# A transformer layer on one core: up to LayerNorm 1, products with a weight piece in two runs, the high part's first and the low part's second

## The chip, the core and the metric

The kernel runs on one core of a Trainium2 chip. A core has five engines with queues of their own: TensorE (PE, matrix products, with its weight loads shown as PEld), VectorE (DVE), ScalarE (ACT), GpSimd (POOL) and SyncE (SP), which here issues the transfers. They wait for each other by semaphores. The metric is the device time of one execution in microseconds (us).

## What is computed

One layer of a diffusion transformer, in float32: 256 latent tokens and 256 context tokens of width 2048, 16 heads of 128. The reference, cut to what matters:

```python
sh1, sc1, g1, sh2, sc2, g2 = ada_mods(c, w_ada[layer], b_ada[layer])
qa, ka, va, qb, kb, vb = mixer_qkv(modulate(x, sh1, sc1), w_in[layer], q_norm_g[layer], k_norm_g[layer], rope)
qac, kac, vac, qbc, kbc, vbc = mixer_qkv(modulate(ctx, csh1, csc1), w_in[layer], q_norm_g[layer], k_norm_g[layer], None)
heads = jnp.concatenate([window_sink_attention(qa, ka, va, kac, vac, sink_logit[layer]),
                         global_attention(qb, kb, vb, kbc, vbc)], axis=-1)
x = layer_norm(DN_ALPHA * x + g1 * (heads @ w_out[layer]), ln1_g[layer], ln1_b[layer])
x = layer_norm(DN_ALPHA * x + g2 * swiglu(modulate(x, sh2, sc2), w_gate[layer], w_up[layer], w_down[layer]),
               ln2_g[layer], ln2_b[layer])
```

`ada_mods` gives shifts, scales and gates: silu of the conditioning vector times `w_ada`. `mixer_qkv` is one product of the modulated tokens with `w_in`, split into queries, keys and values of two head groups.

## The kernel before

**Products in three parts.** A float32 product is made of three products in the faster format F32R. The token operand is split into a high part (a cast) and a low part (the operand minus its high part), and so is the weight. With token parts xh, xl and weight parts hi, lo the kernel adds hi·xh, lo·xh and hi·xl into one accumulator bank of PSUM; `mm3` (L340 to 343) issues them in this order. A weight piece is two blocks of 128 rows by 512 columns: it is loaded by SP into a `raw` buffer, ACT casts `hi` from it (L603), and DVE takes the difference `lo` (L606). The rows of the profile with `hi`, `lo`, `uh`, `ul` (modulated input) and `oTh`, `oTl` (attention output) are these.

**Two halves.** Up to LayerNorm 1 (conditioning columns, q/k/v products, attention, output product) the order of the work is planned: each piece of work is a step of the class `Flow`, with an engine, a supposed duration, the steps that it follows, and the rooms (buffers) that it takes and gives back. `Flow.search` tries orders by a list schedule with random ranks from a fixed seed and keeps the one with the earliest supposed end; `Flow.run` then issues the steps in that order, on all five engines. From LayerNorm 1 on (`pb`, L1462) the code's own order holds: gate and up projections, down projection, LayerNorm 2.

**The steps of a weight piece.** `flow_weights` makes, for each piece, ACT's cast and DVE's difference. The cast takes one room `hl` for both parts (four rooms, `HL_BUFS`); the difference gives back the raw buffer. Pieces loaded ahead for the last output columns (`spare`) take two rooms of the pool `b4` instead. `flow_products` makes one PE step for one piece and one row block of 128 tokens: for one or two weight blocks `mm3`, so three or six products. The step waits for the cast, for the difference (200 ns less), for the operand's high part and its low part (400 ns less), and for the row's step before; it gives back the weight room and both operand rooms. `flow_block` calls it for the q/k/v columns (two row blocks for a query block, four for a key/value block, pieces outside and rows inside), `flow_out` for the output product (two row blocks; with `by_tile` rows outside and pieces inside).

**Work beside them on the planned path.** `flow_columns` (PE, L654) multiplies the conditioning vector with pieces of `w_ada`; `flip` (L755) turns the input, L984 and L937 queries and keys; scores, row maxima (L1031), exponentials (L1043), weighing (L1056), a way through DRAM that turns the probabilities, and the values (L1081) make the attention; L1414 is one more conditioning product at the end of the stage, and `z_flip` (L1445) turns LayerNorm 1's output of the first row block, twice two blocks. Behind that ACT modulates (L1666), casts `u2h` (L1668) and DVE takes `u2l` (L1669) for the first gate products.

Of the kernel before, what the change touches and what calls it, by code (L numbers as in the profile page):

```python
# [14 lines left out]
F32R = mybir.dt.float32r  # L15
# [8 lines left out]
P = 128  # L24
# [4 lines left out]
NT = SEQ // P  # L29
# [237 lines left out]
def dit_layer(ctx: ExitStack, tc: tile.TileContext, x, c, cx, c_ctx, w_ada, b_ada, w_in, q_norm_g,  # L267
              k_norm_g, sink_logit, w_out, ln1_g, ln1_b, w_gate, w_up, w_down, ln2_g, ln2_b,
              rope_cos, rope_sin, out):
    nc = tc.nc  # L270
    x, c, cx = x[0], c, cx[0]
# [4 lines left out]
    whl = ctx.enter_context(tc.tile_pool(name="whl", bufs=HL_BUFS))  # L276
# [63 lines left out]
    def mm3(ps, xh, xl, w, first, last, seeded=False):  # L340
        nc.tensor.matmul(ps, lhsT=xh, rhs=w[0], start=first, stop=False, skip_group_check=seeded)  # L341
        nc.tensor.matmul(ps, lhsT=xh, rhs=w[1], start=False, stop=False, skip_group_check=seeded)  # L342
        nc.tensor.matmul(ps, lhsT=xl, rhs=w[0], start=False, stop=last, skip_group_check=seeded)  # L343
# [28 lines left out]
    araw = ea.enter_context(tc.tile_pool(name="araw", bufs=ADA_BUFS))  # L372
# [172 lines left out]
    def b4(shape, dtype, name):  # L547
        return pa.tile(shape, dtype, tag="b4", name=name, bufs=NB4)
# [39 lines left out]
    def flow_weights(w, k0, nk, c0, width=NB, where=("raw", "araw"), spare=False, small=False, behind=(None, None)):  # L588

        raw, ld = flow_load(w, k0, nk, c0, width, where, small=small)  # L590
        pieces = []
        for s in range(0, nk * width, SUB * NB):
            n = min(SUB * NB, nk * width - s)
            hl = Buf("b4" if spare else "hl")
            hl.rooms = [hl, Buf("b4")] if spare else [hl]

            def cast(hl=hl, s=s, n=n):
                if spare:
                    hl.hi, hl.lo = (b4([P, SUB * NB], F32R, c) for c in ("hi", "lo"))
                else:  # L600
                    hl.hi = whl.tile([P, SUB * NB], F32R, tag="hi", name="hi")
                    hl.lo = whl.tile([P, SUB * NB], F32R, tag="lo", name="lo")
                nc.scalar.copy(hl.hi[:, :n], raw.t[:, s : s + n])  # L603

            def rest(hl=hl, s=s, n=n):
                nc.vector.tensor_tensor(hl.lo[:, :n], raw.t[:, s : s + n], hl.hi[:, :n].bitcast(F32), op=ALU.subtract)  # L606
# [101 lines left out]
    u = {}  # L708
# [94 lines left out]
    def flow_block(g, b, chunks):  # L803


        k0, ng = GROUPS[g]
        kvi = {2: 0, 5: 1}.get(b)
        gi = {0: 0, 1: 1, 3: 2, 4: 3}.get(b)
        rows = range(2 if kvi is None else 4)
        accs = [Buf("acc") for r in rows]  # L810
        sums = [qacc[gi][r] if kvi is None else kvacc[kvi][r // 2][:, r % 2, :] for r in rows]
        ends = {r: flow_seed(accs[r], lambda r=r: sums[r], [evacs[b, r], chunks[0][0][1][0]]) for r in rows} if g >= SEED_G else {}
        done = 0
        for (hl, deps), cols in chunks:
            kk = k0 + done
            base = kk - (kk - k0) % G4
            for r in rows:
                rooms, steps = u[base, r // 2]
                j0 = kk - base

                def operand(j, rooms=rooms, r=r):
                    tt = slice((r % 2) * P, (r % 2) * P + P)
                    return rooms[0].t[:, j, tt], rooms[1].t[:, j, tt]

                xs = [lambda j=j0 + i, f=operand: f(j) for i in range(len(cols))]
                ends[r] = flow_products(hl, deps, steps[j0 // 2], cols, accs[r], xs, done == 0,
                                        done + len(cols) == ng, ends.get(r))
                for m in rooms:
                    m.left += 1
                    ends[r].give.append(m)  # L830
            done += len(cols)
        for r in rows:
            eng = "ACT" if g >= SEED_G or g == 0 and not (r % 2 or b < 2) else "DVE"

            def evac(dst=sums[r], ps=accs[r], eng=eng):
                if eng == "ACT":
                    nc.scalar.copy(dst, ps.t)
                elif g > 0:
                    nc.vector.tensor_add(dst, dst, ps.t)
                else:  # L840
                    nc.vector.tensor_copy(dst, ps.t)

            evacs[b, r] = F.add(eng, 520 if eng == "ACT" else 710 if g < 3 else 615, evac, [ends[r], evacs.get((b, r))], give=[accs[r]])
# [386 lines left out]
    def flow_out(gs, n, by_tile=False):  # L1230
# [9 lines left out]
        def products(gi, i, piece, t):  # L1240
            hl, deps = piece
            rooms, ready = oT[gi]

            def operand(j):
                return rooms[0].t[:, j, t * P : (t + 1) * P], rooms[1].t[:, j, t * P : (t + 1) * P]

            xs = [lambda j=2 * i + c: operand(j) for c in range(2)]
            ends[t] = s = flow_products(hl, deps, ready[t][2 * i : 2 * i + 2], [0, NB], accs[t], xs,
                                        (gi, i) == (gs[0], 0), (gi, i) == (gs[-1], 1), ends.get(t))
            for m in rooms:  # L1250
                m.left += 1
                s.give.append(m)
# [733 lines left out]
```

## Time and profile before

| | |
|---|---|
| Three runs | 1122.13, 1122.73 and 1122.84 us, median 1122.73 |
| Profiled execution, first to last instruction | 1121.0 us |
| Mean granted TensorE clock | 0.996 |
| ACT busy | 598.7 us, 53% |
| High parts up to LayerNorm 1 (L603) | 86 casts, 87.4 us, 1030 ns each |
| Low parts up to LayerNorm 1 (L606) | 86 differences, 101.3 us, 1194 ns each |
| Products hi·xh with the modulated input (L341) | 256, 405 ns each |
| PE idle behind DVE's low part there (L342) | 0.6 us |
| HBM read over the span | 304.07 MB |

The profile shows one execution. Times are us from the first instruction, durations in the groups are means of one instruction in ns. A row of the timeline gives start, duration, engine, line, operation, output<-inputs, and in brackets the idle time before it and what ended it. "PE busy" counts products that overlap each other, and their ends are modelled.

### The profile page before, as it was taken

What the parts mean: (1) busy time and instruction counts of PE and PEld (TensorE: products, weight loads), DVE (VectorE), ACT (ScalarE), POOL (GpSimd) and SP (SyncE); (2) the same over time, 40 slices, a digit from 0 to 9 for tenths busy, and PEclk for the clock granted to TensorE, in tenths of its full rate; (3) what the DMA queues carried; (4) which work ended last, traced back from release to release, by engine and by line L of the source; (5) the groups of instructions that cost most, each with busy time, mean ns of one, the idle gap of its engine ahead of it and who ended that gap; (6) DMA issues with size and microseconds to landing.
All of it is one profiled execution on the core that took longest, in us unless ns stands there. A gap on an engine that the chain in (4) does not pass through costs nothing.

```text
span 1121.0 us, 14130 instructions
## 1 busy us (share of the span) xinstructions
PE 1102.3 (98%) x5213; PEld 883.7 (79%) x5213; DVE 903.4 (81%) x1133; ACT 598.7 (53%) x875; POOL 36.7 (3%) x82
## 2 busy tenths in 40 slices
PE   8999999999999999999999999999999999999995
PEld 6766688777887788888888878888888888888884
DVE  5763589899999888787778697988996987689876
ACT  3341554878685356444475565767766344444442
POOL 1000030110100001000000000000000000000000
PEclk9999999999999999999999999999999999999998
DMA  9999999778999778999956677777776998669742
GB/s 321 394 385 375 393 362 377 247 234 274 345 332 395 249 269 321 348 318 296 336 182 216 223 220 266 234 246 271 228 267 216 329 348 293 228 235 379 287 149 76
DMA packets 178317, 321.26 MB, mean 287 GB/s; under 512 B 8732, under 2 KB 43196, under 8 KB 175943
## 3 DMA queue, kind: packets, MB, share of 16 engines
q1 hardware_dynamic: 177528, 320.03, 81.7%
q8 instruction: 41, 0.67, 0.2%
q10 hardware_dynamic: 720, 0.33, 0.1%
q14 instruction: 28, 0.23, 0.1%
HBM read 304.07 MB, written 16.25 MB: 286 GB/s over the span
## 4 chain that ended last, share of the span: by engine, by line
PE 91%; DMA 3%; DVE 2%; ACT 1%; SPq 1%; issue 0%; ACTq 0%; DVEq 0%
PE acc L341 20%; PE acc L343 20%; PE acc L342 20%; PE wk L342 8%; PE wk L341 8%; PE wk L343 8%; PE wk L1081 2%; PE wk L654 2%; DMA raw<-in_w_in_dram 2%; DVE lo L332 1%; DMA lgb<-in_ln_g_dram 1%; PE wk L755 1%; SPq L569 1%; DMA xt<-in_x_dram 0%; PE wk L1414 0%
## 5 line engine op out<-in xcount | busy, mean ns | idle before, releaser
L331 ACT CAST hi<-raw 128x1024 fp32r<-128x1024 f32 x279 | 290.7, 1054 | 256.4 <-PE acc L343 162.4
L332 DVE TENSOR_TENSOR lo<-raw,hi 128x1024 fp32r<-128x1024 f32 x279 | 336.1, 1220 | 103.6 <-ACT hi L331 101.4
L341 PE MATMUL acc<-hi,u2h 128*128 128x512 f32 x390 | 152.5, 391 | 0.0
L343 PE MATMUL acc<-hi,u2l 128*128 128x512 f32 x390 | 151.7, 390 | 0.7 <-DVE u2l L1669 0.7
L342 PE MATMUL acc<-lo,u2h 128*128 128x512 f32 x390 | 151.8, 389 | 0.0
L603 ACT CAST hi<-raw 128x1024 fp32r<-128x1024 f32 (+1 forms) x86 | 87.4, 1030 | 113.8 <-DMA raw<-in_w_in_dram 63.2
L466 DVE SCALAR_TENSOR_TENSOR adav<-raw,cs,adav 128x512 f32<-128x512 f32 (+1 forms) x128 | 121.4, 949 | 8.4 <-DMA raw<-in_w_ada_dram 4.9
L606 DVE TENSOR_TENSOR lo<-raw,hi 128x1024 fp32r<-128x1024 f32 (+1 forms) x86 | 101.3, 1194 | 16.3 <-ACT hi L603 15.5
L341 PE MATMUL acc<-hi,uh 128*128 128x512 f32 x256 | 103.7, 405 | 1.3 <-ACT uh L769 0.8
L342 PE MATMUL wk<-lo,u2h 128*128 128x512 f32 x264 | 103.1, 390 | 0.5 <-DVE lo L332 0.5
L343 PE MATMUL wk<-hi,u2l 128*128 128x512 f32 x264 | 102.7, 389 | 0.0
L341 PE MATMUL wk<-hi,u2h 128*128 128x512 f32 x264 | 102.2, 389 | 0.0
L342 PE MATMUL acc<-lo,uh 128*128 128x512 f32 x256 | 100.5, 392 | 0.6 <-DVE lo L606 0.6
L343 PE MATMUL acc<-hi,ul 128*128 128x512 f32 x256 | 100.1, 391 | 0.4 <-DVE ul L784 0.4
L341 PE MATMUL acc<-hi,hTh 128*128 128x512 f32 x236 | 92.0, 390 | 0.4 <-ACT acc L1901 0.4
L342 PE MATMUL acc<-lo,hTh 128*128 128x512 f32 x236 | 91.8, 389 | 0.0
L343 PE MATMUL acc<-hi,hTl 128*128 128x512 f32 x236 | 91.8, 389 | 0.0
L343 PEld LDWEIGHTS acc<-hi,u2l 128*128 128x128 f32 x390 | 73.2, 188 | 16.2 <-DVE u2l L1669 1.1
L341 PEld LDWEIGHTS acc<-hi,u2h 128*128 128x128 f32 x390 | 73.2, 188 | 16.1 <-ACT u2h L1668 0.8
L342 PEld LDWEIGHTS acc<-lo,u2h 128*128 128x128 f32 x390 | 73.2, 188 | 15.1
L341 PEld LDWEIGHTS acc<-hi,uh 128*128 128x128 f32 x256 | 48.1, 188 | 19.0 <-issue 5.6
L342 PEld LDWEIGHTS wk<-lo,u2h 128*128 128x128 f32 x264 | 49.5, 188 | 12.0 <-DVE lo L332 1.8
(277 smaller groups left out, 1748.0 us busy)
## 6 DMA issues: line engine op xcount, KB each, us to landing
raw<-in_w_ada_dram SPq DMA_DIRECT2D x70, 1024.0 KB, 7.7
raw<-in_w_gate_dram SPq DMA_DIRECT2D x44, 1024.0 KB, 6.7
raw<-in_w_up_dram SPq DMA_DIRECT2D x44, 1024.0 KB, 5.6
raw<-in_w_down_dram SPq DMA_DIRECT2D x44, 1024.0 KB, 5.8
raw<-in_w_ada_dram SPq DMA_DIRECT2D x48, 512.0 KB, 5.9
raw<-in_w_in_dram SPq DMA_DIRECT2D x18, 1024.0 KB, 11.0
raw<-in_w_out_dram SPq DMA_DIRECT2D x16, 1024.0 KB, 6.5
pd<-hx SPq DMA_DIRECT2D x64, 128.0 KB, 3.4
```

Of the source, the lines that this page charges most:

```text
L331: nc.scalar.copy(hi[:, :n], raw[:, s : s + n])
L332: nc.vector.tensor_tensor(lo[:, :n], raw[:, s : s + n], hi[:, :n].bitcast(F32), op=ALU.subtract)
L341: nc.tensor.matmul(ps, lhsT=xh, rhs=w[0], start=first, stop=False, skip_group_check=seeded)
L342: nc.tensor.matmul(ps, lhsT=xh, rhs=w[1], start=False, stop=False, skip_group_check=seeded)
L343: nc.tensor.matmul(ps, lhsT=xl, rhs=w[0], start=False, stop=last, skip_group_check=seeded)
L466: nc.vector.scalar_tensor_tensor(a[:, c : c + piece], raw[:, f : f + piece], cs[:, 4 * (g * (G4 * NB // w) + j) + 2, None], a[:, c : c + p ...
L569: nc.sync.dma_start(room.t, w[k0 * P : (k0 + 1) * P, c0 : c0 + width])
L603: nc.scalar.copy(hl.hi[:, :n], raw.t[:, s : s + n])
L606: nc.vector.tensor_tensor(hl.lo[:, :n], raw.t[:, s : s + n], hl.hi[:, :n].bitcast(F32), op=ALU.subtract)
L654: nc.tensor.matmul(bank.t[32 * j : 32 * j + 32, :width], lhsT=cs[:, 4 * k + 2 - 2 * i : 4 * k + 34 - 2 * i], rhs=raw.t[:, c * width : (c + ...
L755: nc.tensor.transpose(ps.t[:, (j * 2 + t) * P : (j * 2 + t + 1) * P], src, ident)
L1081: nc.tensor.matmul(o_ps.t[:, : 2 * P].rearrange("p (g q) -> p g q", q=32), lhsT=v, rhs=pv[:, k], start=k == 0, stop=k == 3)
```

## The change

The room `hl` becomes two, `hi` and `lo`, four of each as before. The cast takes the high room only; the difference takes the low room when DVE comes to it, and the tile is made there. The PE step of a piece and a row block becomes two: the high run (hi·xh and hi·xl for each block, two or four products) and the low run (lo·xh, one or two). The high run waits for the cast and for the operand's parts (the low one 200 ns less), and gives back the high room and the operand's low room; the low run waits for its own high run and for the difference, and gives back the low room and the operand's high room. In `flow_block` the high runs of all row blocks of a piece are named first and then the low runs, in `flow_out` too, except with `by_tile`, where each low run follows its high run. The order in which they are named is a rank for the planner, not the order of the program. The rest of the code, past LayerNorm 1 too, is the same; its lines move by up to 12.

```diff
-    F = Flow({"raw": RAW_BUFS, "araw": ADA_BUFS, "hl": HL_BUFS, "acc": 4, ...
+    F = Flow({"raw": RAW_BUFS, "araw": ADA_BUFS, "hi": HL_BUFS, "lo": HL_BUFS, "acc": 4, ...
...
-            hl = Buf("b4" if spare else "hl")
-            hl.rooms = [hl, Buf("b4")] if spare else [hl]
+            hl = Step()
+            hl.rooms = [Buf("b4"), Buf("b4")] if spare else [Buf("hi"), Buf("lo")]
...
-            a = F.add("ACT", 60 + 0.87 * n, cast, [ld, behind[0]], hl.rooms)
-            b = F.add("DVE", 60 + 1.06 * n, rest, [a, behind[1]], give=[raw])
+            a = F.add("ACT", 60 + 0.87 * n, cast, [ld, behind[0]], hl.rooms[:1])
+            b = F.add("DVE", 60 + 1.06 * n, rest, [a, behind[1]], hl.rooms[1:], [raw])
...
-        after = [deps[0], (deps[1], 200), ready[0], (ready[1], 400), prev]
-        return F.add("PE", 681 * len(cols), fn, after, [ps] if first and not seed else [], list(hl.rooms))
+        def high():
+            if first and not seed:
+                ps.t, ps.seeded = acc_bank(), False
             for i, (c, x) in enumerate(zip(cols, xs)):
+                for j, h in enumerate(x()):
+                    nc.tensor.matmul(ps.t, lhsT=h, rhs=hl.hi[:, c : c + NB], start=first and not seed and i == j == 0,
+                                     stop=False, skip_group_check=ps.seeded)
+
+        def low():
+            for i, (c, x) in enumerate(zip(cols, xs)):
+                nc.tensor.matmul(ps.t, lhsT=x()[0], rhs=hl.lo[:, c : c + NB], start=False,
+                                 stop=last and i == len(cols) - 1, skip_group_check=ps.seeded)
+
+        a = F.add("PE", 454 * len(cols), high, [deps[0], ready[0], (ready[1], 200), prev],
+                  [ps] if first and not seed else [], hl.rooms[:1])
+        return a, lambda: F.add("PE", 227 * len(cols), low, [a, deps[1]], [], hl.rooms[1:])
...
-                ends[r] = flow_products(hl, deps, steps[j0 // 2], cols, accs[r], xs, done == 0,
-                                        done + len(cols) == ng, ends.get(r))
-                for m in rooms:
-                    m.left += 1
-                    ends[r].give.append(m)
+                a, lows[r] = flow_products(hl, deps, steps[j0 // 2], cols, accs[r], xs, done == 0,
+                                           done + len(cols) == ng, ends.get(r))
+                rooms[1].left += 1
+                a.give.append(rooms[1])
+            for r in rows:
+                rooms = u[base, r // 2][0]
+                ends[r] = lows[r]()
+                rooms[0].left += 1
+                ends[r].give.append(rooms[0])
```

**The opening on TensorE.** The first products of the kernel, with the first piece of w_in; `acc`, `hi`, `lo`, `uh` and `ul` carry the numbers of their tiles. Before:

```order
L391 MATMUL wk_96<-ident_70 128x128 x4
L341 MATMUL acc_245<-hi_221,uh_233 128x512
L342 MATMUL acc_245<-lo_222,uh_233 128x512
L343 MATMUL acc_245<-hi_221,ul_234 128x512
L341 MATMUL acc_253<-hi_221,uh_233 128x512
L342 MATMUL acc_253<-lo_222,uh_233 128x512
L343 MATMUL acc_253<-hi_221,ul_234 128x512
```

Now (L629 are high products, L634 low ones):

```order
L391 MATMUL wk_96<-ident_70 128x128 x4
L629 MATMUL acc_246<-hi_223,uh_235 128x512
L629 MATMUL acc_246<-hi_223,ul_236 128x512
L629 MATMUL acc_251<-hi_223,uh_235 128x512
L629 MATMUL acc_251<-hi_223,ul_236 128x512
L634 MATMUL acc_246<-lo_233,uh_235 128x512
```

The product with the low part of the input has moved from the third place to the second, the one with the low part of the weight to the fifth.

**The piece of w_in near 102 us on TensorE.** Behind two groups of conditioning products comes the first piece of the next w_in load. Before:

```order
L654 MATMUL wk_938<-raw_903,cs_106 32x512 x4
L654 MATMUL wk_938<-raw_958,cs_106 32x512 x4
L1381 MATMUL wk_1009<-ident_70,lrow_153 128x32
L341 MATMUL acc_1011<-hi_999,uh_832 128x512
L342 MATMUL acc_1011<-lo_1000,uh_832 128x512
L343 MATMUL acc_1011<-hi_999,ul_833 128x512
```

Now the same place ends its sixteen high products (four row blocks, four each, the last four shown) with:

```order
L629 MATMUL acc_1022<-hi_991,ul_864 128x512
L629 MATMUL acc_1027<-hi_991,uh_863 128x512
L629 MATMUL acc_1027<-hi_991,ul_864 128x512
L629 MATMUL acc_1027<-hi_991,uh_863 128x512
L629 MATMUL acc_1027<-hi_991,ul_864 128x512
L634 MATMUL acc_1008<-lo_1006,uh_839 128x512 x2
```

The first product with the low part stood second; now sixteen others are ahead of it.

**VectorE in the attention stretch, now.** Rows with what each waits for: `lo` are differences of weight pieces, `hx` turned probabilities, `m` row maxima, `nm` and `es` what the exponentials need.

```order
L603 TENSOR_TENSOR lo<-raw,hi 128x1024 [waits PE_49]
L1070 STREAM_TRANSPOSE hx<-pr 128x4x4x32 [waits Activation_49]
L1038 TENSOR_REDUCE m<-wk 128x1
L603 TENSOR_TENSOR lo<-raw,hi 128x1024 [waits DMAHW5_49,PE_49,Activation_49]
L1043 SCALAR_TENSOR_TENSOR nm<-m,nsink 128x2 [waits DVE_49]
L1044 TENSOR_TENSOR es<-nm,nsink 128x2 [waits DVE_49]
```

The waits for PE in the rows of `lo` stood with ACT's cast of the same piece before; of 86 such rows 36 have one now, and 4 had one.

**The end of the stage on TensorE.** The last output products, the conditioning products L1414 (now L1426) and the flips of LayerNorm 1's output L1445 (now L1457), up to the first gate product. Before:

```order
L343 MATMUL acc_3493<-hi_3345,oTl_3260 128x512
L1414 MATMUL wk_3664<-raw_3535,cs_106 32x512 x4
L1445 MATMUL wk_3670<-ident_70,xt_76 128x128 x2
L1414 MATMUL wk_3664<-raw_3551,cs_106 32x512 x4
L1445 MATMUL wk_3679<-ident_70,xt_76 128x128 x2
L1414 MATMUL wk_3664<-raw_3567,cs_106 32x512 x4
L1414 MATMUL wk_3664<-raw_3584,cs_106 32x512 x4
L341 MATMUL acc_3724<-hi_3614,u2h_3696 128x512
```

Now:

```order
L1426 MATMUL wk_3655<-raw_3530,cs_106 32x512 x4
L634 MATMUL acc_3509<-lo_3442,oTh_3254 128x512 x2
L1426 MATMUL wk_3655<-raw_3550,cs_106 32x512 x4
L1426 MATMUL wk_3655<-raw_3567,cs_106 32x512 x4
L1426 MATMUL wk_3655<-raw_3583,cs_106 32x512 x4
L1457 MATMUL wk_3684<-ident_70,xt_76 128x128 x2
L1457 MATMUL wk_3688<-ident_70,xt_76 128x128 x2
L341 MATMUL acc_3724<-hi_3594,u2h_3696 128x512
```

All conditioning products have moved ahead of both flips. ACT's first modulation reads `wk_3670` before and `wk_3688` now.

More of the change, by code (lines that the diff above doesn't have):

```diff
@@ L537, in dit_layer @@
     fill(pa, 448)
-    F = Flow({"raw": RAW_BUFS, "araw": ADA_BUFS, "hl": HL_BUFS, "acc": 4, "wk": 4, "b4": NB4, "t2k": T2K},
+    F = Flow({"raw": RAW_BUFS, "araw": ADA_BUFS, "hi": HL_BUFS, "lo": HL_BUFS, "acc": 4, "wk": 4, "b4": NB4, "t2k": T2K},
              {"SP": 1800.0, "PE": 6300.0, "ACT": 5100.0, "DVE": 4200.0, "POOL": 4000.0})
@@ L593, in flow_weights @@
             n = min(SUB * NB, nk * width - s)
-            hl = Buf("b4" if spare else "hl")
-            hl.rooms = [hl, Buf("b4")] if spare else [hl]
+            hl = Step()
+            hl.rooms = [Buf("b4"), Buf("b4")] if spare else [Buf("hi"), Buf("lo")]
             def cast(hl=hl, s=s, n=n):
[L598 to L602, printed above, removed]
+                hl.hi = b4([P, SUB * NB], F32R, "hi") if spare else whl.tile([P, SUB * NB], F32R, tag="hi", name="hi")
                 nc.scalar.copy(hl.hi[:, :n], raw.t[:, s : s + n])
             def rest(hl=hl, s=s, n=n):
+                hl.lo = b4([P, SUB * NB], F32R, "lo") if spare else whl.tile([P, SUB * NB], F32R, tag="lo", name="lo")
                 nc.vector.tensor_tensor(hl.lo[:, :n], raw.t[:, s : s + n], hl.hi[:, :n].bitcast(F32), op=ALU.subtract)
-            a = F.add("ACT", 60 + 0.87 * n, cast, [ld, behind[0]], hl.rooms)
-            b = F.add("DVE", 60 + 1.06 * n, rest, [a, behind[1]], give=[raw])
+            a = F.add("ACT", 60 + 0.87 * n, cast, [ld, behind[0]], hl.rooms[:1])
+            b = F.add("DVE", 60 + 1.06 * n, rest, [a, behind[1]], hl.rooms[1:], [raw])
             pieces.append((hl, (a, b)))
@@ L625, in flow_products @@
         seed = first and prev is not None
-        def fn():
+        def high():
             if first and not seed:
@@ L630, in fn @@
             for i, (c, x) in enumerate(zip(cols, xs)):
-                xh, xl = x()
-                mm3(ps.t, xh, xl, (hl.hi[:, c : c + NB], hl.lo[:, c : c + NB]),
-                    first and not seed and i == 0, last and i == len(cols) - 1, ps.seeded)
-        after = [deps[0], (deps[1], 200), ready[0], (ready[1], 400), prev]
-        return F.add("PE", 681 * len(cols), fn, after, [ps] if first and not seed else [], list(hl.rooms))
+                for j, h in enumerate(x()):
[8 more added lines that the diff above has]
+        return a, lambda: F.add("PE", 227 * len(cols), low, [a, deps[1]], [], hl.rooms[1:])
     last_load, first_sum = [], []
@@ L816, in flow_block @@
             base = kk - (kk - k0) % G4
+            lows = {}
             for r in rows:
@@ L1247, in products, with finish @@
             xs = [lambda j=2 * i + c: operand(j) for c in range(2)]
[L1248 to L1252, printed above, removed]
+            a, low = flow_products(hl, deps, ready[t][2 * i : 2 * i + 2], [0, NB], accs[t], xs,
+                                   (gi, i) == (gs[0], 0), (gi, i) == (gs[-1], 1), ends.get(t))
+            rooms[1].left += 1
+            a.give.append(rooms[1])
+            def finish():
+                ends[t] = s = low()
+                rooms[0].left += 1
+                s.give.append(rooms[0])
+            return finish
         if by_tile:
@@ L1256, in flow_out @@
                 for p in pieces:
-                    products(*p, t)
+                    products(*p, t)()
         else:
             for p in pieces:
-                for t in range(NT):
-                    products(*p, t)
+                run([products(*p, t) for t in range(NT)])
         def finish(t):
```

## The prediction

> **What bounds the kernel now.** I read the page's shares and its chain first, then the busy time by stretch, then the order of time around every place where TensorE (PE) stands still.
>
> ```profile
> PE 1102.3 (98%) x5213; PEld 883.7 (79%) x5213; DVE 903.4 (81%) x1133; ACT 598.7 (53%) x875; POOL 36.7 (3%) x82
> PE 91%; DMA 3%; DVE 2%; ACT 1%; SPq 1%; issue 0%; ACTq 0%; DVEq 0%
> 100.00:120.00 20.00, 19.44 (x115) 11.99 (x113) 6.14 (x10) 2.58 (x3) 0.00 (x0) 1.00 1.05 405
> 160.00:180.00 20.00, 20.00 (x90) 16.57 (x89) 19.61 (x24) 13.72 (x19) 2.02 (x4) 1.00 1.04 414
> 260.00:280.00 20.00, 18.51 (x84) 14.72 (x83) 19.03 (x39) 17.23 (x42) 0.00 (x0) 1.00 0.81 265
> ```
>
> TensorE sets the time: 98% busy, 91% of the chain. In the stretches (columns: us; busy us of PE, PEld, DVE, ACT, POOL; granted clock; DMA share; GB/s) the clock is 1.00 throughout. Between 160 and 180 us VectorE (DVE) is busy for 19.61 of 20 us too, and the DMA share is full: nothing has much room.
>
> A busy PE hides small waits, though. A 512-column product is shown 0.39 us long, but the next begins after 0.227:
>
> ```profile
> 265.22 0.39 PE L343 MATMUL acc<-hi,oTl 128*128 128x512 f32 x1
> ...
> 267.94 0.39 PE L343 MATMUL acc<-hi,oTl 128*128 128x512 f32 x1
> 269.62 0.50 PE L341 MATMUL wk<-kTh,qTh 128*128 128x512 f32 x1 [1.29 <-ACT pr L1043]
> ...
> 271.11 0.40 PE L342 MATMUL acc<-lo,oTh 128*128 128x512 f32 x1
> 271.71 0.50 PE L343 MATMUL acc<-hi,oTl 128*128 128x512 f32 x1 [0.20 <-DVE oTl L1093]
> 272.04 0.40 PE L341 MATMUL acc<-hi,oTh 128*128 128x512 f32 x1
> ```
>
> Twelve products stand between the first two rows: 2.72 / 12 = 0.227 us each. So a wait is read from start to start. The step from 267.94 to 269.62 is 1.68 us, 1.45 too long, though the row says 1.29; and a product behind a wait is followed after 0.33, 0.11 too late. The second wait (271.11 to 271.71) costs 0.60 - 0.23 + 0.11 = 0.48. The two make 1.45 + 0.11 + 0.48 = 2.0 us, the largest loss of the attention stretch. The change can win such waits and nothing else: it takes no product away.
>
> **The change, part by part.** *Same work.* A triple (high·high, low·high, high·low) becomes two products in the high run and one in the low run, each 0.227 us, with as many casts, differences and transfers. Weight loads stay one for each product (x5213 against x5213) and lie beside products (16.57 of 20 us). Zero from the rows; the bounds are zero too, as no form of instruction is new.
>
> *The order is drawn anew.* The planner is a seeded random search over its steps. There are more steps now, so all five engines' orders up to LayerNorm 1 differ, also where no weight piece is involved. The sum therefore goes by places.
>
> *The opening*, from the rows of before:
>
> ```profile
> 14.14 0.50 PE L341 MATMUL acc<-hi,uh 128*128 128x512 f32 x1 [0.79 <-ACT uh L769]
> 14.48 0.41 PE L342 MATMUL acc<-lo,uh 128*128 128x512 f32 x1
> 14.83 0.43 DVE L784 TENSOR_TENSOR ul<-uf,uh 128x256 fp32r<-128x256 f32 x1
> 15.31 0.50 PE L343 MATMUL acc<-hi,ul 128*128 128x512 f32 x1 [0.42 <-DVE ul L784]
> 16.09 0.69 DVE L841 COPY kvacc<-acc 128x512 f32<-128x512 f32 x1
> 16.69 3.16 DVE L606 TENSOR_TENSOR lo<-raw,hi 128x1024 fp32r<-128x1024 f32 x3
> 20.50 0.50 PE L341 MATMUL acc<-hi,uh 128*128 128x512 f32 x1 [0.43 <-DVE kvacc L841]
> 21.39 0.32 PE L654 MATMUL wk<-raw,cs 128*32 128x128 f32 x4
> ```
>
> In before the first wait is for the low part of the input (`ul`, ready at 14.83 + 0.43 = 15.26), and the low weight product runs ahead of it. Now `ul` is needed by the second product: at 15.31 one product is done instead of two. The other wait, for an accumulator that DVE empties, comes a product group earlier: DVE now takes the three differences before its first copy, so from 16.09, where the copy began, they end at 16.09 + 3.16 = 19.25 and the copy at 19.25 + 0.69 = 19.95; PE waits from 19.3 to about 20.1, and six products are left. The conditioning products (L654 in before) then start at 20.1 + 0.34 + 5 × 0.227 + 0.1 = 21.65 instead of 21.39. I take **+0.3**; bounds -0.3 (both waits half as long) and +0.9 (both in full again).
>
> *The late w_in piece at 102 us.*
>
> ```profile
> 100.89 1.99 ACT L603 CAST hi<-raw 128x1024 fp32r<-128x1024 f32 x2 [11.58 <-DMA raw<-in_w_in_dram]
> ...
> 101.97 2.36 DVE L606 TENSOR_TENSOR lo<-raw,hi 128x1024 fp32r<-128x1024 f32 x2 [1.00 <-ACT hi L603]
> ...
> 102.20 0.49 PE L341 MATMUL acc<-hi,uh 128*128 128x512 f32 x1
> 103.25 0.50 PE L342 MATMUL acc<-lo,uh 128*128 128x512 f32 x1 [0.56 <-DVE lo L606]
> 103.59 0.40 PE L343 MATMUL acc<-hi,ul 128*128 128x512 f32 x1
> ```
>
> The high part is there just in time; the difference takes 1.2 us more and PE stands. In the new order sixteen high products (16 × 0.227 = 3.6 us) stand between, so the wait goes: 103.59 - 102.20 - 2 × 0.227 = 0.94. I take **-0.9**; bounds -0.9 and 0 (if the piece lands so much later that PE waits for the high part). What would be late next is the second difference at 101.97 + 2.36 = 104.3; its products come later still.
>
> *The attention stretch.* Here the change adds a wait. The low room was taken together with the high room, by ScalarE's (ACT's) cast; now DVE takes it when it comes to the difference. In the order with waits 36 of the 86 differences wait for PE, where 4 did. Queued behind each are the row maxima, the subtractions for the next operands and the copies out of accumulators, and PE waits for all of these. ACT is relieved: the high room comes back before the low run.
>
> ```profile
> ACT hi L603 <- PE acc L343: 41.4, 27, 10.7
> ...
> 265.65 1.06 ACT L603 CAST hi<-raw 128x1024 fp32r<-128x1024 f32 x1 [0.67 <-PE acc L343]
> 266.60 1.33 ACT L1056 ACTIVATE pr<-pr,ll 128x512 f32<-128x512 f32 x2
> ...
> 268.72 0.76 ACT L1043 ACTIVATE pr<-wk,nm,qsc 128x512 f32<-128x512 f32 x1
> ```
>
> The first row (view of waits: us, times, longest) prices such a wait at 41.4 / 27 = 1.5 us of the waiting engine. The others show when it reaches PE: ACT stood 0.67 us for a room at 265.65, its exponential came at 268.72, and the score product of 269.62 waited for the bank. The old 2.0 us go with the old order. Against them I set new ones, since DVE has 0.39 us free in 20 (160 to 180 us) and now waits more often. The nearest rows are these two waits, so I take nearly their like back, 1.8: **-0.2**; bounds -2.0 (none comes back) and +4.0 (three such events).
>
> *The end of the stage.*
>
> ```profile
> 386.76 0.44 PE L1445 MATMUL wk<-ident,xt 128*128 128x128 f32 x2
> 387.13 1.07 PE L1414 MATMUL wk<-raw,cs 128*32 128x512 f32 x8
> 388.13 0.44 PE L1445 MATMUL wk<-ident,xt 128*128 128x128 f32 x2
> 388.50 1.92 PE L1414 MATMUL wk<-raw,cs 128*32 128x512 f32 x16
> 390.35 0.50 PE L341 MATMUL acc<-hi,u2h 128*128 128x512 f32 x1
> ...
> 395.25 0.60 PE L1445 MATMUL wk<-ident,xt 128*128 128x128 f32 x4
> 395.60 0.49 PE L341 MATMUL acc<-hi,u2h 128*128 128x512 f32 x1
> ...
> 387.30 0.81 ACT L1666 ACTIVATE uf<-wk,mB,mA 128x128 f32<-128x128 f32 x2 [3.57 <-PE wk L1445]
> 388.14 0.41 ACT L1668 CAST u2h<-uf 128x256 fp32r<-128x256 f32 x1
> ...
> 388.95 0.41 DVE L1669 TENSOR_TENSOR u2l<-uf,u2h 128x256 fp32r<-128x256 f32 x1
> ```
>
> In before the flip of LayerNorm 1's first tile stands between the conditioning products (L1414), which cover ACT's modulation: flip at 386.76, `u2h` at 388.55, `u2l` at 389.36, first gate product at 390.35 without a wait. In the new order all four groups of conditioning products stand ahead of both flips, and the flip that is used first comes second. With the flips at T: second flip T + 0.22, `u2h` by the same distance (388.55 - 386.76 = 1.79) at T + 2.01, product at T + 2.07. Four flips alone let it start at T + 0.35 (395.25 to 395.60). So PE stands 1.7 us, and again 0.35 for `u2l` (needed at T + 2.64, there by T + 2.01 + 0.81 + 0.06, then a restart of 0.11). Two runs of conditioning products instead of three give back 0.15. I take **+1.9**; bounds +1.0 (ACT starts as soon as half the flip is there) and +2.5. The cover that is gone are the 3.6 us from 386.76 to 390.35; nothing else stands there.
>
> *Sum against the profiled span*: 1121.0 + 0.3 - 0.9 - 0.2 + 1.9 = 1122.1. The median of the runs shown, 1122.73, is 1.7 above the span; with that, **1123.8 us**. Past LayerNorm 1 the code is the same and bound by products, so I carry the shift through unchanged.
>
> **Rivals.**
>
> *A queue that waits for its own low room* (clearly slower). DVE is nearly full, PE needs its results, and now it waits for PE 36 times. Where PE is late, the low run is late, the difference stands at the head of DVE's queue, and the row maximum behind it makes PE later still. One such round costs PE what the one at 267.94 did, 1.45 + 0.11 + 0.48 = 2.0 us. It decides once more than about 2.5 rounds occur: three of them besides the 1.8 above give 1123.8 + 3 × 2.0 - 1.8 = 1128.0. For it: 19.61 of 20 us busy. Against it: the planner counts these rooms, and of ACT's 27 waits for rooms the rows above show one that reached PE. The Trainium skill, TensorE: Matmul & The Clock Gate, section on the array of 32×32 blocks, says that VectorE and ScalarE take their queues strictly in order while TensorE may pull weight loads ahead. By that rule a waiting difference holds all behind it and this rival's round is real; the trace agrees with it in the rows at 265.65 to 268.72, on ACT.
>
> *The waits go and the tail is harmless* (faster). If the attention stretch keeps none of its 2.0 us and the tail costs its lower bound: 1122.7 + 0.3 - 0.9 - 2.0 + 1.0 = 1121.1; with no tail wait at all, 1120.1. For it: the high run gives DVE 0.9 to 1.8 us more (4 to 8 products) before its result is needed. Against it: the flips stand last in the order, which no timing changes.
>
> *The change does little*: in the opening most low runs stand right behind their own high run, as before in effect; then only the tail differs, 1122.7 + 1.9 = 1124.6, no change by the measure below.
>
> **How the numbers follow.** A measurement of this kernel tells about 0.2% (2.2 us) from no change: 1120.5 to 1125.0. Chances: the forecast 0.42 (it holds 1122.0 to 1125.5; 0.37 of it lies within 0.2%, 0.05 above), little change 0.13 (all within), the faster rival 0.13 (0.08 of it clearly faster), the queue rival 0.32 (0.31 clearly slower). That makes faster 0.08, same 0.37 + 0.13 + 0.05 + 0.01 = 0.56, slower 0.36. The range takes the faster rival's 1120.1 and, above, the attention bound: 1123.8 + 4.0 + 0.2 = 1128.0. About 0.05 is left out below, 0.13 above. The likeliest case's own range is 1122.0 to 1125.5.
>
> **What would show each step.** Right: no step over 0.3 us between the first products of the piece near 102 us; a step of 1.5 to 2 us between the last flip and the first gate product, put down to ACT; the opening's conditioning products near 21.6. Wrong: DVE idle behind PE by more than some 5 us in all before its differences, with steps of over 1 us on PE between 200 and 380 us (the queue rival); a first gate product less than 0.6 us behind the flips; or a stretch past 400 us whose length differs from before by over 0.5 us, since I carry the shift through.

## The result and the profile after

The changed kernel takes 1126.42 us (median of 8 runs, 1123.92 to 1128.65) against 1122.78 us (1121.65 to 1123.93) for the kernel before: a ratio of 1.0033, 95% interval 1.0022 to 1.0043. It is 3.64 us slower, clear of the 0.2% that can be told. The forecast was 1123.8 us; the time lies inside the range of 1120.1 to 1128.0 us, but outside the 1122.0 to 1125.5 us given to the likeliest case. The outcome "clearly slower" had a chance of 0.36, "no change" 0.56. The profiled execution has a span of 1125.4 us (before 1121.0) and the same clock, 0.996.

The shares of busy time and the chain of the changed kernel, then its stretches (columns as before; the last row is the kernel before, for comparison):

```profile
PE 1103.0 (98%) x5213; PEld 883.3 (78%) x5213; DVE 902.6 (80%) x1133; ACT 597.2 (53%) x875; POOL 39.3 (3%) x82
PE 88%; DMA 5%; DVE 4%; ACT 2%; issue 1%; SPq 0%; ACTq 0%; DVEq 0%
```

```profile
100.00:120.00 20.00, 20.00 (x115) 12.49 (x113) 6.13 (x8) 2.58 (x3) 0.00 (x0) 1.00 1.02 383
260.00:280.00 20.00, 20.00 (x95) 16.62 (x94) 19.02 (x41) 16.10 (x39) 3.36 (x11) 1.00 0.90 306
340.00:360.00 20.00, 18.24 (x73) 13.34 (x72) 17.64 (x18) 8.61 (x13) 0.00 (x0) 1.00 1.05 402
...
340.00:360.00 20.00, 20.00 (x86) 15.86 (x85) 18.08 (x20) 8.58 (x13) 0.00 (x0) 1.00 1.05 399
```

The same 5213 products and the same clock, so the time is waits. The two stretches in which PE stood before (100 to 120 and 260 to 280 us) are full now; 340 to 360 us, which was full, is at 18.24. PE's waits by what ended them (us in all, times, longest):

```profile
PE wk L656 <- DMA raw<-in_w_ada_dram: 2.5, 3, 1.9
PE acc L629 <- DVE oTl L1100: 1.7, 2, 1.5
...
PE acc L341 <- ACT u2h L1680: 1.4, 1, 1.4
PE wk L1457 <- DVE xt L1235: 1.3, 1, 1.3
```

Where the difference arises is read best by putting each run's PE at the same point of its work: the costs of the instructions issued so far are added up, one price per shape, and the start times at equal sums compared. In the table each entry is us later than the profiled execution of before at that point; the runs x1 to x7 are the experiments below.

| PE's work done, us (time in before) | after | x3 | x4 | x5 | x6 | x7 | x1 | x2 |
|---|---|---|---|---|---|---|---|---|
| 10 (21.1) | 0.0 | -0.4 | +0.8 | +0.8 | -0.4 | +1.3 | +0.9 | +1.0 |
| 80 (95.1) | +2.3 | -0.1 | +1.7 | +0.4 | +1.5 | +1.3 | +1.3 | +1.7 |
| 90 (106.5) | +1.3 | -1.0 | +0.7 | -0.5 | +0.6 | +1.5 | +0.5 | +0.7 |
| 190 (209.0) | +1.7 | -0.8 | +1.0 | -0.5 | +0.7 | +1.5 | +1.7 | +1.3 |
| 200 (219.0) | +2.8 | +0.2 | +2.0 | +0.6 | +1.5 | +1.5 | +1.7 | +2.4 |
| 260 (281.7) | +0.3 | -2.2 | -0.5 | -1.9 | -0.9 | +1.5 | +3.8 | +1.2 |
| 310 (331.7) | +1.2 | -0.8 | +0.2 | -1.2 | -0.1 | +1.5 | +5.3 | +2.3 |
| 360 (381.9) | +4.0 | +1.2 | +0.7 | -1.0 | +0.6 | +1.6 | +6.3 | +7.2 |
| 380 (404.1) | +6.3 | +1.1 | +2.9 | -1.1 | +0.4 | +5.4 | +7.9 | +9.7 |
| 600 (624.0) | +6.3 | +1.1 | +3.0 | -1.1 | +0.5 | +5.4 | +8.0 | +9.7 |
| 650 (675.3) | +4.9 | -0.2 | +1.6 | -2.4 | -0.9 | +4.0 | +6.6 | +8.3 |

The column "after" has gains (80 to 90, 200 to 260) and losses (190 to 200, 260 to 360, 360 to 380). Up to 310 the columns after, x3, x4 and x5 have one and the same order, and yet lie up to 2.5 us apart, nearly all of it from the first 80 us. That part differs from execution to execution: PE's longest wait for a `w_ada` transfer was 1.9 us in after and 0.3 us in x3. What repeats is the change from row to row.

### The profile page after: what moved, and what is told of

It reads as the page before. It is cut to its first block, busy times and chain, and to the rows that moved or that the text cites. A ratio compares the mean times of both kernels' runs of the same rounds, so it can differ in the third digit from the quotient of the medians.

```text
span 1125.4 us, 14148 instructions
## 1 busy us (share of the span) xinstructions
PE 1103.0 (98%) x5213; PEld 883.3 (78%) x5213; DVE 902.6 (80%) x1133; ACT 597.2 (53%) x875; POOL 39.3 (3%) x82
## 4 chain that ended last, share of the span: by engine, by line
PE 88%; DMA 5%; DVE 4%; ACT 2%; issue 1%; SPq 0%; ACTq 0%; DVEq 0%
PE acc L341 13%; PE acc L343 13%; PE acc L342 13%; PE acc L629 12%; PE wk L341 8%; PE wk L342 8%; PE wk L343 8%; PE acc L634 6%; DMA raw<-in_w_ada_dram 2%; DMA raw<-in_w_in_dram 2%; PE wk L656 2%; PE wk L1088 2%; DVE lo L603 1%; ACT hi L599 1%; DMA cxt<-in_ctx_dram 0%
## 5 line engine op out<-in xcount | busy, mean ns | idle before, releaser
L466 DVE SCALAR_TENSOR_TENSOR adav<-raw,cs,adav 128x512 f32<-128x512 f32 (+1 forms) x128 | 121.3, 948 | 12.8 <-DMA raw<-in_w_ada_dram 10.7
L603 DVE TENSOR_TENSOR lo<-raw,hi 128x1024 fp32r<-128x1024 f32 (+1 forms) x86 | 101.7, 1199 | 20.0 <-ACT hi L599 19.6
L629 PE MATMUL acc<-hi,uh 128*128 128x512 f32 x256 | 102.8, 402 | 1.1 <-ACT uh L771 0.8
L629 PE MATMUL acc<-hi,ul 128*128 128x512 f32 x256 | 100.3, 392 | 0.7 <-DVE ul L786 0.7
L634 PE MATMUL acc<-lo,uh 128*128 128x512 f32 x256 | 76.7, 398 | 0.0
L629 PEld LDWEIGHTS acc<-hi,uh 128*128 128x128 f32 x256 | 48.1, 188 | 18.3 <-issue 5.2
L341 PEld LDWEIGHTS wk<-hi,u2h 128*128 128x128 f32 x264 | 49.5, 188 | 10.4
```

The lines of the kernel that those rows point to most:

```text
L466: nc.vector.scalar_tensor_tensor(a[:, c : c + piece], raw[:, f : f + piece], cs[:, 4 * (g * (G4 * NB // w) + j) + 2, None], a[:, c : c + p ...
L629: nc.tensor.matmul(ps.t, lhsT=h, rhs=hl.hi[:, c : c + NB], start=first and not seed and i == j == 0, stop=False, skip_group_check=ps.seeded)
L634: nc.tensor.matmul(ps.t, lhsT=x()[0], rhs=hl.lo[:, c : c + NB], start=False, stop=last and i == len(cols) - 1, skip_group_check=ps.seeded)
```

## The experiments

The planner's order is a list of steps, so a kernel can be told to issue a given list instead of searching. Such kernels were made by one edit, and their lists differ in the places told below:

```diff
-        for s, s.start, pools in self.search()[0]:
-            for b, b.pool in zip(s.take, pools):
-                pass
+        for i in ORDER:
+            s = self.steps[i]
+            for b in s.take:
+                b.pool = "araw" if i in ARAW else b.pools[0]
             s.fn()
```

The added list moves the lines: rows of x1 to x6 that are from `flow_products` bear L704 or L705 for high products and L709 or L710 for low ones, others are 75 or 76 lines further on (64 in x7).

**x1: the change on the old order.** The changed code, issued in the order of the kernel before:

```diff
-L341 MATMUL acc<-hi,uh 128x512
-L342 MATMUL acc<-lo,uh 128x512
-L343 MATMUL acc<-hi,ul 128x512
-L341 MATMUL acc<-hi,uh 128x512
-L342 MATMUL acc<-lo,uh 128x512
-L343 MATMUL acc<-hi,ul 128x512
+L705 MATMUL acc<-hi,uh 128x512
+L705 MATMUL acc<-hi,ul 128x512
+L705 MATMUL acc<-hi,uh 128x512
+L705 MATMUL acc<-hi,ul 128x512
+L710 MATMUL acc<-lo,uh 128x512
+L705 MATMUL acc<-hi,uh 128x512
```

The rows are the start of TensorE's order. A low run stands behind the last high run of its piece, or, where something that needs its bank follows earlier, just ahead of that.

> The change without the new draw: the steps of the changed kernel in the order of the kernel before, each high run where the old product step stood, the low runs of a piece behind its last high run, both rooms apart. Theory A (the new order costs, not the two runs): the 0.94 us wait near 102 us goes and nothing comes, 1120.5 to 1122.8 us, ratio at most 1.000. Theory B (two runs or the low part's own room cost): most of the 3.6 us is there, 1125 us or more, ratio 1.002 or more.

Measured: 1131.17 us against 1122.85 us for before, ratio 1.0080 (1.0057 to 1.0102). Theory A missed: it expected no loss at all. Theory B's "1125 us or more" holds to the letter, but a loss of 8.3 us is more than twice the 3.6 us that it was to explain. The first PE waits of this run:

```profile
PE wk L1533 <- DVE xt L1311: 1.6, 1, 1.6
...
PE wk L417 <- ACT pr L1126: 1.4, 1, 1.4
```

No place stands out; some eight waits of 0.5 to 1.6 us lie in opening, attention and end (the column x1 climbs at each). It would fit that what was timed for a high-low-high triple now comes at other times (a bank is complete only with the low run, and the operand's low part is asked for by the second product, not the third), but no run separates this. The gain of the prediction is there as well (80 to 90: 0.8 us).

**x2: the two runs undone, on the new order.** Each low step is put directly behind its own high step, or behind its difference where that comes later; the list is otherwise that of the changed kernel.

```diff
 L705 MATMUL acc<-hi,uh 128x512
 L705 MATMUL acc<-hi,ul 128x512
-L705 MATMUL acc<-hi,uh 128x512
-L705 MATMUL acc<-hi,ul 128x512
 L710 MATMUL acc<-lo,uh 128x512
+L705 MATMUL acc<-hi,uh 128x512
+L705 MATMUL acc<-hi,ul 128x512
+L710 MATMUL acc<-lo,uh 128x512
```

> The new order with the two runs undone: each low run stands directly behind its own high run (or behind its difference, where that is issued later); all else in the order of the changed kernel. Theory A: still slow, 1125.5 to 1127.5 us, the stalls near 32, 348 and 394 us are there as before, and up to 0.9 us comes back as a wait for a late difference. Theory B: back at the kernel before, 1122 to 1124 us.

Measured: 1130.88 us, ratio 1.0069 (1.0052 to 1.0087): 4.5 us slower than the changed kernel. Theory B falls, since undoing the runs does not undo the loss; theory A's 1125.5 to 1127.5 us was too low. With x1 it says that either way of issuing the products costs 4 to 8 us under an order that was drawn for the other, in the one arrangement of the low runs that was tried for each.

**The draw.** The planner's seed is 312 in both kernels. Two more draws of each:

```diff
-    SEED, SIGMA, MOVES, DRAWS, JITTER = 312, 600.0, 1000, 5, 0.04
+    SEED, SIGMA, MOVES, DRAWS, JITTER = 313, 600.0, 1000, 5, 0.04
```

> The kernel before with another seed of the planner (313 instead of 312): same code, another order. Theory C (the draw decides, the two runs as such cost nothing): seeds of one code lie as far apart as before and after do, 1119 to 1129 us for either code, and the two codes overlap. Theory D (the two runs cost with any order drawn for them): the seeds of the kernel before stay within 1.5 us of 1122.8 us and every changed one is above every one of before.

> As the run with seed 313, a further draw for the kernel before (seed 314). Theory C: anywhere from 1119 to 1129 us. Theory D: 1121.3 to 1124.3 us.

> The changed kernel with seed 313: same code, another order. Theory C: anywhere from 1119 to 1129 us, at least one of the changed seeds at or under 1123 us. Theory D: 1125 to 1128 us, above every draw of the kernel before.

> The changed kernel with seed 315, a further draw. Theory C: anywhere from 1119 to 1129 us. Theory D: 1125 to 1128 us.

| Seed | code before | code after |
|---|---|---|
| 312 | 1123.05 (in the same comparison) | 1126.42 |
| 313 | 1127.13, ratio 1.0038 (1.0024 to 1.0051) | 1124.53, ratio 1.0014 (1.0001 to 1.0027) |
| 314 | 1130.71, ratio 1.0064 (1.0043 to 1.0085) | |
| 315 | | 1126.41, ratio 1.0028 (1.0018 to 1.0037) |
| mean | 1127.0 | 1125.8 |

Theory D falls on both counts: the draws of the kernel before spread over 7.7 us, and the medians of all three changed ones lie below two of the three of before. Theory C's picture holds, though not its numbers to the letter: one draw of before passes 1129 us, and no changed one came under 1123 us. Three draws a side cannot tell whether the two runs are better or worse by a microsecond; they do show that the kernel before stands at the fast end of its own draws, by 4 and 8 us, and that any change that makes the planner draw again starts from there.

**x3: the flips.** The order of the changed kernel with LayerNorm 1's flips of the first tile moved forward (rows of TensorE's order):

```diff
-L1501 MATMUL wk<-raw,cs 32x512 x12
-L1532 MATMUL wk<-ident,xt 128x128 x4
+L1501 MATMUL wk<-raw,cs 32x512 x4
+L1532 MATMUL wk<-ident,xt 128x128 x2
+L1501 MATMUL wk<-raw,cs 32x512 x4
+L1532 MATMUL wk<-ident,xt 128x128 x2
+L1501 MATMUL wk<-raw,cs 32x512 x4
```

> The changed kernel with one thing moved: LayerNorm 1's two flips of the first tile stand between the last conditioning products instead of behind them all. Theory A: the step of 1.65 us between the last flip and the first gate product goes, and the time falls by 1.2 to 2.0 us, to 1124.4 to 1125.2 us. Rival: VectorE's LayerNorm of the second tile is late anyway and takes it back, 1126 to 1127 us.

Measured: 1123.55 us, ratio 1.0005 (0.9993 to 1.0016): 2.9 us less than the changed kernel, more than the 1.2 to 2.0 us expected. First the place in the changed kernel (timeline, PE and then DVE):

```profile
391.04 2.78 PE L1426 MATMUL wk<-raw,cs 128*32 128x512 f32 x24
393.75 0.66 PE L1457 MATMUL wk<-ident,xt 128*128 128x128 f32 x4
395.79 0.50 PE L341 MATMUL acc<-hi,u2h 128*128 128x512 f32 x1 [1.38 <-ACT u2h L1680]
396.12 0.40 PE L342 MATMUL acc<-lo,u2h 128*128 128x512 f32 x1
396.36 0.40 PE L343 MATMUL acc<-hi,u2l 128*128 128x512 f32 x1
...
402.14 0.63 PE L1457 MATMUL wk<-ident,xt 128*128 128x128 f32 x4 [1.29 <-DVE xt L1235]
...
392.59 0.69 DVE L1290 BATCH_NORM_STATS2 stats<-xt 128x6 f32<-128x512 f32 x1
395.76 0.43 DVE L1681 TENSOR_TENSOR u2l<-uf,u2h 128x256 fp32r<-128x256 f32 x1 [2.48 <-ACT u2h L1680]
...
397.25 0.25 DVE L1213 BATCH_NORM_AGGREGATE mv<-stats 128x2 f32<-128x24 f32 x1
...
399.16 0.75 DVE L466 SCALAR_TENSOR_TENSOR adav<-raw,cs,adav 128x512 f32<-128x512 f32 x1
...
400.01 0.74 DVE L466 SCALAR_TENSOR_TENSOR adav<-raw,cs,adav 128x512 f32<-128x512 f32 x1
...
400.80 0.74 DVE L466 SCALAR_TENSOR_TENSOR adav<-raw,cs,adav 128x512 f32<-128x512 f32 x1
401.46 0.54 DVE L1235 TENSOR_SCALAR xt<-xt,mv,ly 128x512 f32<-128x512 f32 x1
```

There are two waits. PE stands for `u2h`, as predicted. And PE's next flip, at 402.14, stands for the normalised rows of the second row block (401.46), which come late for two reasons. DVE stands 2.48 us for the same `u2h` before it can take `u2l`, with the mean and variance of that block (397.25) queued behind. By the rule of the Trainium skill that the prediction weighed (TensorE: Matmul & The Clock Gate, section on the array of 32×32 blocks: VectorE takes its queue strictly in order) a waiting head delays what is queued behind it; these rows agree: the statistics that the mean needs are done at 393.28 us, and it starts only behind the second `u2l`, at 397.25. And between the mean and the normalised rows stand three modulation sums (L466) that the kernel before takes behind them:

```profile
390.22 0.26 DVE L1206 BATCH_NORM_AGGREGATE mv<-stats 128x2 f32<-128x24 f32 x1
...
392.76 0.55 DVE L1228 TENSOR_SCALAR xt<-xt,mv,ly 128x512 f32<-128x512 f32 x1
394.78 1.54 DVE L466 SCALAR_TENSOR_TENSOR adav<-raw,cs,adav 128x512 f32<-128x512 f32 x2 [1.48 <-DMA adav<-in_b_ada_dram]
```

From the mean to the normalised rows are 2.54 us there and 4.21 us in the changed kernel, 1.67 us more than before and more than the wait of 1.29 us. These sums are of the code past the planned path, which is the same in both kernels and names them after all normalised rows. VectorE's order there is neither the code's nor the same in both; why, no run shows. Over the thirteen profiled kernels the wait follows them: with none (before, its seed 313) or two (x3, x5, x6) between mean and rows PE does not wait for the rows, with three or four (all others) it waits 1.3 to 1.9 us. One of these is x1, which has the flips of the kernel before and no wait for `u2h`, but four sums: its first row above is this wait. So the sums can make it without the wait for `u2h`; no run moves them alone.

In x3 neither wait is left. Besides the flips, one of the three sums has moved behind the normalised rows in it:

```profile
389.25 0.44 PE L1532 MATMUL wk<-ident,xt 128*128 128x128 f32 x2
389.62 1.06 PE L1501 MATMUL wk<-raw,cs 128*32 128x512 f32 x8
390.62 0.44 PE L1532 MATMUL wk<-ident,xt 128*128 128x128 f32 x2
390.99 1.07 PE L1501 MATMUL wk<-raw,cs 128*32 128x512 f32 x8
391.98 0.50 PE L416 MATMUL acc<-hi,u2h 128*128 128x512 f32 x1
```

**x7: the same flips put last in the kernel before**, the counter-test:

```diff
-L1478 MATMUL wk<-raw,cs 32x512 x4
-L1509 MATMUL wk<-ident,xt 128x128 x2
-L1478 MATMUL wk<-raw,cs 32x512 x4
-L1509 MATMUL wk<-ident,xt 128x128 x2
-L1478 MATMUL wk<-raw,cs 32x512 x8
+L1478 MATMUL wk<-raw,cs 32x512 x16
+L1509 MATMUL wk<-ident,xt 128x128 x4
```

> The kernel before with LayerNorm 1's two flips of the first tile behind all conditioning products, the first-used one second, as the changed kernel has them; nothing else. By the prediction's term for the end of the stage 1.9 us more, 1124.7 us (bounds +1.0 and +2.5); by the changed kernel's trace 2.25 us more, 1125.1 us. Rival (the order around them hides it in this kernel): within 0.5 us of 1122.9 us.

Measured: 1126.39 us against 1122.64 us, ratio 1.0034 (1.0017 to 1.0052): 3.75 us, more than either number expected (the interval reaches down to 1.9 us), and as much as the whole change. Between points 360 and 380 of the work it loses 3.8 us in the trace, by the same two waits:

```profile
392.94 0.50 PE L405 MATMUL acc<-hi,u2h 128*128 128x512 f32 x1 [1.39 <-ACT u2h L1732]
...
399.91 0.63 PE L1509 MATMUL wk<-ident,xt 128*128 128x128 f32 x4 [1.91 <-DVE xt L1292]
```

It is not the flips alone, though. In this run VectorE takes four modulation sums between the mean and the normalised rows, where the kernel before takes none. What the flips cost without them was not measured.

**x4: the low part at 348 us.** Rows of VectorE's order, against that of the changed kernel:

```diff
-L541 SCALAR_TENSOR_TENSOR adav<-raw,cs,adav 128x1024
-L1175 TENSOR_TENSOR oTl<-wk,oTh 128x2x128
-L541 SCALAR_TENSOR_TENSOR adav<-raw,cs,adav 128x1024
+L1175 TENSOR_TENSOR oTl<-wk,oTh 128x2x128
+L541 SCALAR_TENSOR_TENSOR adav<-raw,cs,adav 128x1024 x2
```

> The changed kernel with one thing moved: on VectorE the low part of an attention output (oTl) that PE waits for at 348 us is taken before the modulation sum that waits for a w_ada transfer, not behind it. Theory A: the step of 1.88 us on PE near 348 us falls to under 0.5 us and the time by 1.2 to 1.8 us, to 1124.6 to 1125.2 us. Rival: PE is held by the next late thing in the same place (the sum, the next difference), 1126 to 1127 us.

Measured: 1125.29 us, ratio 1.0019 (1.0008 to 1.0031): 1.1 us less than the changed kernel, just short of the 1.2 expected. The intervals of the two ratios (1.0008 to 1.0031 and 1.0022 to 1.0043) overlap, so the time alone does not show this gain; the trace does (310 to 360: +0.5 instead of +2.8). In the changed kernel DVE takes a modulation sum (L466) that waits for a `w_ada` transfer, and `oTl` stands behind it; PE steps from 347.96 to 349.85 us, 1.89 instead of about 0.23:

```profile
347.96 0.39 PE L629 MATMUL acc<-hi,oTh 128*128 128x512 f32 x1
349.85 0.50 PE L629 MATMUL acc<-hi,oTl 128*128 128x512 f32 x1 [1.49 <-DVE oTl L1100]
...
348.17 1.28 DVE L466 SCALAR_TENSOR_TENSOR adav<-raw,cs,adav 128x1024 f32<-128x1024 f32 x1 [0.50 <-DMA raw<-in_w_ada_dram]
349.37 0.42 DVE L1100 TENSOR_TENSOR oTl<-wk,oTh 128x256 fp32r<-128x256 f32 x1
```

In x4 `oTl` is done before the sum, and PE goes on after 0.24 us:

```profile
346.02 0.40 PE L704 MATMUL acc<-hi,oTh 128*128 128x512 f32 x1
346.26 0.39 PE L704 MATMUL acc<-hi,oTl 128*128 128x512 f32 x1
...
344.44 0.42 DVE L1175 TENSOR_TENSOR oTl<-wk,oTh 128x256 fp32r<-128x256 f32 x1
```

**x5 and x6: the moves together.** x5 has the moves of x3 and x4. x6 has a third, on ScalarE, at the step of 0.91 us that PE makes at 213 us:

```diff
-L674 CAST hi<-raw 128x1024
 L1125 ACT_TABLE_LOAD
 L1125 ACTIVATE pr,ll<-wk,nm 128x512 x2
+L674 CAST hi<-raw 128x1024
```

> Both single moves in the changed kernel, the flips between the conditioning products and oTl ahead of the sum. If the stalls are places of the order and each costs for itself, the gains found for each add up: 1126.4 - 2.9 - 1.1 = 1122.4 us (1121.5 to 1123.2), as fast as the kernel before. Rival (one wait behind them all, VectorE's end of the stage, takes back what is won earlier): 1123.5 us or more, no better than the flips alone.

> As the run with two moves, and a third: near 211 us ScalarE's two exponentials stand ahead of a weight cast that waited 3.09 us for its high room, not behind it. If that queue made the step of 0.91 us on PE at 213 us: that step falls to 0.25 us and the time by a further 0.5 to 1.0 us, to 1121.4 to 1121.9 us, faster than the kernel before. Rival: the cast that is now later makes its high run late, no gain, 1122.4 us.

Measured: x5 1122.73 us, ratio 1.0002 (0.9993 to 1.0012); x6 1122.92 us, ratio 1.0000 (0.9991 to 1.0009). The first two gains add up, 3.7 us of the 4.0 expected. The third gave nothing. In the changed kernel the place reads:

```profile
213.25 0.39 PE L629 MATMUL acc<-hi,ul 128*128 128x512 f32 x1
214.15 0.50 PE L341 MATMUL wk<-kTh,qTh 128*128 128x512 f32 x1 [0.52 <-ACT pr L1050]
...
210.95 1.06 ACT L599 CAST hi<-raw 128x1024 fp32r<-128x1024 f32 x1 [3.09 <-PE acc L629]
212.03 1.28 ACT L1050 ACT_TABLE_LOAD   x1
```

The cast stood 3.09 us for its high room, with the table load and the exponentials queued behind. In x6 PE's step there is gone, and a new one of 1.01 us stands 5 us later, for the copy that fills an accumulator (`acc`, L690). In x5 the place's first product (212.16 us in x6) starts at 211.06 us, the same copy at 216.40 (217.36 in x6), and the product that needs it at 217.06 (218.01):

```profile
212.16 0.39 PE L704 MATMUL acc<-hi,ul 128*128 128x512 f32 x1
212.39 0.39 PE L416 MATMUL wk<-kTh,qTh 128*128 128x512 f32 x1
...
217.00 0.40 PE L704 MATMUL acc<-hi,ul 128*128 128x512 f32 x1
218.01 0.50 PE L704 MATMUL acc<-hi,uh 128*128 128x512 f32 x1 [0.61 <-ACT acc L690]
```

Counted from that first product, the copy starts after 5.34 us in x5 and after 5.20 us in x6, nearly where it was. PE gets to it earlier by what it won at the step, and waits for it: of 0.7 us, 0.15 is left. No version beat the kernel before by more than its interval.

## Why the prediction missed the size

- **Same work: right.** 5213 products before and after, and clock 0.996 in both.
- **Opening, +0.3: not to be told.** The timeline of the changed kernel has the conditioning products at 21.37 us, where 21.65 was forecast and 21.39 stood before, and behind them the wait of 1.90 us for a transfer:

```profile
21.37 1.96 PE L656 MATMUL wk<-raw,cs 128*32 128x128 f32 x64
...
32.65 1.07 PE L656 MATMUL wk<-raw,cs 128*32 128x256 f32 x16 [1.90 <-DMA raw<-in_w_ada_dram]
```

  Both waits behind the term are there: PE's second product comes 1.17 us after its first (14.23 to 15.40 us), for the operand's low part, and at 19.79 us it has stood for an accumulator, in a step of 0.63 us. But runs of the same order are from 0.4 us earlier to 0.8 us later at the first of these points, and lie 2.4 us apart at 95 us. A term of 0.3 us is below that.
- **The w_in piece, -0.9: right.** The first high products of the late piece start without a wait at 104.29 us, while DVE is at its differences until 105.64; the low run comes at 108.05 us:

```profile
103.29 2.35 DVE L603 TENSOR_TENSOR lo<-raw,hi 128x1024 fp32r<-128x1024 f32 x2
104.29 0.50 PE L629 MATMUL acc<-hi,uh 128*128 128x512 f32 x1
...
108.05 1.52 PE L634 MATMUL acc<-lo,uh 128*128 128x512 f32 x6
```

  Between points 80 and 90 the changed kernel gains 1.0 us, x1 to x6 gain 0.8 to 1.0, and x7, which has the old order, does not.
- **Attention stretch, -0.2: the step that failed.** The old 2.0 us went as forecast (points 200 to 260: +2.8 to +0.3). But the term "I take nearly their like back, 1.8" was too small. By the table the new losses are 1.5 us from point 90 to 200 (about 1.0 of it at 213 us), 0.9 from 260 to 310 and 2.8 from 310 to 360, with the step at 348 us the largest: 5.2 us. So from point 90 to 360 the changed kernel is 2.7 us longer than before, x3 2.2, where 0.2 less was forecast; x4, without the step at 348 us, comes out even. The loss lies within the bounds of -2.0 and +4.0, and the time lies in the forecast's range through this upper bound: the kind of loss was named, its size was not. The 1.8 was read from the two worst waits of before, an order that came out faster than all five other draws, by 1.5 to 7.7 us.
- **End of the stage, +1.9: right place, half of the mechanism.** 2.3 us in the trace of the changed kernel, 2.9 us by x3, 3.75 us when put into the kernel before. The wait for `u2h` is there (2.04 us from the flips at 393.75 to 395.79, where 2.07 was forecast). The 0.35 for `u2l` is not: the products follow each other after 0.33 and 0.24 us. In its place came the wait for the second row block's normalised rows, a step of 1.68 us that no term of the prediction holds: DVE stood for `u2h`, and three modulation sums had moved ahead of the rows. Most of a wait of before for a later `u2l` (0.68 us at 398.59 us) went in turn.
- **Past LayerNorm 1, carried unchanged: right from point 380 to 600, but not in every execution.** The code there is the same, though VectorE's order at its start is not (the sums above). All columns of the table stay as they are from point 380 to 600, then all drop by 1.3 or 1.4 us at once, x7 with the old order too. It is before's own execution that lost there. Its VectorE waited for a LayerNorm gain from DRAM, and PE, some 16 us later, for a difference of VectorE's; that the one led to the other is argued. x5's execution lost in its turn near 791 us, by the wait in the last row.

```profile
636.78 1.29 DVE L1491 SCALAR_TENSOR_TENSOR xt<-xt,lgb 128x512 f32<-128x512 f32 x2 [4.77 <-DMA lgb<-in_ln_g_dram]
...
653.80 0.50 PE L342 MATMUL wk<-lo,u2h 128*128 128x512 f32 x1 [0.37 <-DVE lo L332]
...
PE wk L417 <- DVE lo L407: 1.9, 2, 1.7
```

In sum: -0.9, +2.3 to +2.7 and +2.3 make 3.7 to 4.1 us, against 3.64 measured; the terms are read from single executions, the 3.64 from medians. The other forecasts: "the change does little" (1124.6 us) had the tail as the only difference, and x7 shows that the tail alone, flips and sums, can make all of it. The queue rival (1128.0 us) is nearest in time and wrong in its cause. Its sign was DVE idle behind PE before its differences by over 5 us:

```profile
DVE lo L603 <- ACT hi L599: 19.6, 12, 6.7
```

This is all that the view of waits has for the differences in the changed kernel: 19.6 us behind casts and nothing behind PE. With seed 315 it has the most of all the kernels run:

```profile
DVE lo L603 <- PE acc L634: 1.0, 2, 0.8
```

So the 36 differences that name PE as a wait found the low room free almost always. What was real in that rival is the strict queue, with other heads: a sum that waits for its transfer (348 us), a `u2l` that waits for ACT (395.76 us), a cast that waits for its high room (211 us). The faster rival's argument, that the high run gives DVE more time, is seen at the w_in piece only.

What stays open is whether two runs are in themselves better or worse than triples. Three draws a side give means of 1125.8 and 1127.0 us, with 7.7 us between draws. Larger spare rooms for the low part were not tried. Open too is how the tail's loss divides between the flips and the modulation sums.

## What to carry to other kernels

Where a search or a seed sets the order, a change of its steps is two changes: its own, and a new draw. Price the draw from a few other seeds of the old code before reading the change from one pair of kernels, and expect a tuned order to lose when it is drawn again. In a new order look first for an instruction that waits at the head of a strict queue, and follow what is queued behind it to its own consumer. Two flips, moved across one to three groups of conditioning products, with the modulation sums that moved along, were worth 2.9 to 3.75 us here, up to as much as the whole change. And compare every engine's order also where the code is the same.

## What the runs showed of the hardware

- One and the same order runs with differences of up to 2.4 us in its first 95 us (the rows at point 80: +2.3, -0.1, +1.7 and +0.4 us for after, x3, x4 and x5), with PE's longest wait for a `w_ada` transfer 1.9 us in after and 0.3 us in x3. A profiled execution alone can't price a term of 1 us there.
- A wait for a room need not reach TensorE: of 46.3 us of such waits of ScalarE's casts in the changed kernel (41.4 before), one step on PE was found behind them, of 0.91 us at 213 us.
